# First expert's gate and up weights multiplied whole in float32; the slots for parts filled from the second expert's gate on

## The chip, the cores and the metric

The kernel runs on one core of a Trainium2 chip. Times are microseconds of device time for one execution; three runs of the kernel before gave a median of 1385.62 us (1385.28 to 1387.55). A difference between two kernels is stated with its sign, minus for faster.

The engines are named as in the profile: PE (matrix products, TensorE), DVE (VectorE), ACT (ScalarE), POOL (GpSimd), SP (SyncE, which issues DMAs). A matrix product accumulates in PSUM. The two levels of TensorE's clock are 2.4 and 1.2 GHz; a granted clock of 1.00 in the profile is the higher one, 0.50 the lower.

## The reference

Two layers of an encoder over 512 tokens of width 1024. Each layer is an attention part (four kinds of heads, their outputs joined and multiplied by `w_out`, added to `x`) and a mixture of 16 experts, of which each token uses two of one group. The experts' part is what the change touches:

```python
def hier_moe(h, wg, bg, we, be, w_gate, w_up, w_down):
    ...
    gate = jnp.sum(jax.nn.one_hot(expert_id, N_EXPERTS, dtype=jnp.float32) * (g_w * e_w)[..., None], axis=1)
    y = jnp.zeros_like(t)
    for e in range(N_EXPERTS):
        hid = jax.nn.silu(t @ w_gate[e]) * (t @ w_up[e])
        y = y + gate[:, e:e + 1].astype(t.dtype) * (hid @ w_down[e])
    return y.reshape(b, s, d)
```

`w_gate` and `w_up` are 1024x512 per expert, `w_down` 512x1024, all float32.

## The kernel before

**Precision in parts.** A float32 operand is cut into a high part (`hi`, an ACT copy into the rounded type fp32r) and a low part (`lo`, raw minus hi, on DVE or POOL): function `split` (L143 to L145). `mm3` (L264 to L269) then forms a product from three fp32r matmuls: hi times xh, lo times xh, hi times xl.

**Weights.** The class `Weights` streams all weights in pieces of 512 KB, numbered in the order of use. `load` (L183, L186) sends a piece into a raw room when one is free, on SP's queue; `split` turns the next loaded piece into parts when one of HL = 6 slots for parts is free, and gives its room back; `free` gives the slots back once the products have been issued. In a layer of the mixture the pieces follow `MOE_ORDER`: four of the first expert's gate, four of its up, four of the second's gate, four of the first's down, the second's up, the third's gate, and so on. In the tables of instructions, raw_1933, raw_3162, raw_3707 and raw_3709 are the first expert's gate in layer 0, raw_3711 to raw_3720 its up, and raw_3722 is the first piece of the second expert's gate.

**Experts.** Every expert works on at most CAP = 96 gathered tokens. For each, DVE makes four one-hot tiles (`oh`, L341), PE turns them into a list (`pli`, L1389), DVE reduces that to row numbers and weights, POOL gathers the rows (`xg`, L1401), PE turns them (`ptg`, L1413) and ACT and DVE split them into `xh` and `xl`. Then come gate (`pg`), up (`pu`), the product of both (`sg`), down (`pd`) and a scatter that adds to the output. The first expert's rows come another way: PE collects them while the attention ends (`acc`, L1142), and `turn` splits that straight from PSUM.

**What sets the order.** Towards the end of the attention a table, `TAIL`, says which steps are issued after which unit of work. Its words that matter here: `sV` and `sG` split the next piece on DVE or POOL if it is loaded and a slot is free (and do nothing otherwise), `c`, `o`, `d`, `e`, `f` with a digit are steps of the joined output and the router for a block of tokens, `T` is `turn` of the first expert, `K` the routing weights (24 small operations on DVE and two on ACT), `m` clears a buffer on POOL, `B` stores the last block of `x`, `S` gathers the second expert's rows, `O` is the branch for lists longer than CAP (not taken here), `q` copies constants on POOL. After the table the loop over `MOE_ORDER` issues the rest.

Of the kernel before, what the change touches and what calls it, by code (L numbers as in the profile page):

```python
# [11 lines left out]
FT = mybir.dt.float32  # L12
# [3 lines left out]
AF = mybir.ActivationFunctionType  # L16
# [3 lines left out]
S = 512  # L20
# [27 lines left out]
        69: "T K m sG B O q sG S"}  # L48
# [14 lines left out]
def hybrid_encoder(ctx: ExitStack, tc: tile.TileContext, I: dict, out: bass.AP, depth=2, dbg=None):  # L63
# [83 lines left out]
    class Weights:  # L147
# [4 lines left out]
        def __init__(self):  # L152
            self.spec, self.raw, self.hl, self.where = [], {}, {}, {}
            self.loaded = self.done = self.used = 0
            self.moe_pools = []
            self.held, self.paused = 0, False
            self.spare, self.spare_upto = [], 0

# [30 lines left out]

        def split(self, upto, E=V):  # L190

            while self.done < min(upto, self.loaded) and self.done < self.used + self.HL - self.held:
# [5 lines left out]
                r = self.where.pop(u)  # L198
                if isinstance(r, bass.AP):
                    self.spare.append(r)  # L200
# [13 lines left out]
        def free(self, upto):  # L214
            for u in range(self.used, upto):
                del self.hl[u]
            self.used = upto
# [25 lines left out]
    for l in range(depth):  # L243
# [10 lines left out]
        for e, m in MOE_ORDER:  # L254
# [3 lines left out]
            elif (e, m) == (NE - 1, 'u'):  # L258

                add_piece((l, e, m), I[src][l, e], 0, FF // 2, 8, 4, moe=True, parts=2, pairs=True)  # L260
            else:
                add_piece((l, e, m), I[src][l, e], 0, FF, 8, 2, moe=True, pairs=True)

# [59 lines left out]
    for layer in range(depth):  # L323
# [32 lines left out]
        with ExitStack() as c2:  # L356
# [431 lines left out]
            with ExitStack() as c3:  # L788
# [356 lines left out]
                def list_rows():  # L1145

                    pl = ps.tile([128, 512], FT, name="pli", tag="tr")
                    for t in range(NT):
# [7 lines left out]
                              p=route, x=pick, s=lambda E: W.split(W.done + 1, E), w=warm)  # L1156
# [151 lines left out]
        with ExitStack() as c2:  # L1308
# [69 lines left out]
            class Expert:  # L1378
# [25 lines left out]
                def turn(self, turned=None):  # L1404
                    self.xh = sm.tile([128, 8, CAP], FR, name="xh", bufs=2)
                    self.xl = sm.tile([128, 8, CAP], FR, name="xl", bufs=2)
                    for k in range(0, 8, 4):
                        if turned:
                            pt = turned[k // 4]
                        else:  # L1410
                            pt = ps.tile([128, 4, CAP], FT, name="ptg", tag="tr")
                            for j in range(4):
                                PE.transpose(pt[:, j], self.g[:CAP, (k + j) * 128:(k + j + 1) * 128], ident[:CAP, :CAP])  # L1413
                        split(self.xh[:, k:k + 4], self.xl[:, k:k + 4], pt)

                def gu(self, m, i, w):

                    if i == 0:
                        pool, tag = (pq, "pv") if m == 'u' else (ps, "mm") if self is not X[0] else (pq, "sc")
                        p = pool.tile([128, FF], FT, name="p" + m, tag=tag)  # L1420
                        setattr(self, 'p' + m, p[:CAP])
                    mm3(getattr(self, 'p' + m), [(self.xh[:, k], self.xl[:, k]) for k in (2 * i, 2 * i + 1)],
# [257 lines left out]
```

## Time and profile before

| | |
|---|---|
| median of three runs | 1385.62 us |
| the profiled execution | 1387.39 us, its span 1385.6 us |
| mean granted clock | 0.969 |
| busy, share of the span | PE 93%, DVE 78%, ACT 63%, POOL 26% |
| mixture stage, layer 0 | 386.8 to about 698 us |
| mixture stage, layer 1 | 1062.6 to about 1374 us |

A row of the timeline gives start, duration, engine, line, operation, output and inputs, how often in a row, and in brackets how long the engine had been idle before and what ended that. The durations of matmuls overlap, so one costs what lies between its start and the next one's. A float32 matmul stands in the trace as two records, an fp32r one as one.

### The profile page before, as it was taken

To read this page: it belongs to the slowest core of one execution; us is meant where nothing else is said; L and a number is where in the kernel's file an instruction comes from. 1 tells how busy PE (TensorE), PEld (TensorE's weight loads), DVE (VectorE), ACT (ScalarE), POOL (GpSimd) and SP (SyncE) were. 2 spreads that over 40 slices of the span, in tenths; PEclk is the share of its full clock that TensorE was granted. 3 is DMA by queue.
4 is the path that set the end of the run, shared out by engine and by line. 5 is a ranking of instruction groups with operands and counts; after the bars stand their busy time and mean duration, and the time that the engine had idled before them with its cause. 6 is when DMAs were issued, how large, how long until landed. Compare 5 with 4: busy or idle time off the path is not lost.

```text
span 1385.6 us, 21247 instructions
## 1 busy us (share of the span) xinstructions
PE 1293.8 (93%) x7222; PEld 1013.9 (73%) x7222; DVE 1087.5 (78%) x2108; ACT 876.4 (63%) x1439; POOL 358.5 (26%) x582
## 2 busy tenths in 40 slices
PE   8998899999969999999989998999998899999996
PEld 6776688888836666766777886888886566667674
DVE  4636776878688999999876488687876799999994
ACT  3443357766357888888744454676644588888884
POOL 4204324323422111111041152431345021111120
PEclk8999999999979999999999999999997899999999
DMA  7332251012699999999454223200176899999960
GB/s 198 116 97 62 83 177 51 18 60 108 257 334 292 370 363 373 359 361 332 124 136 123 91 77 79 69 28 28 62 296 222 292 351 368 370 363 366 367 206 13
DMA packets 100575, 278.46 MB, mean 201 GB/s; under 512 B 19465, under 2 KB 30521, under 8 KB 100456
## 3 DMA queue, kind: packets, MB, share of 16 engines
q1 hardware_dynamic: 89528, 247.95, 50.4%
q0 software_dynamic: 10352, 27.41, 7.9%
q10 hardware_dynamic: 576, 1.64, 0.4%
q8 instruction: 59, 0.97, 0.3%
q14 instruction: 60, 0.49, 0.1%
HBM read 264.34 MB, written 24.81 MB: 209 GB/s over the span
## 4 chain that ended last, share of the span: by engine, by line
PE 25%; DVE 17%; DMA 12%; issue 11%; ACT 4%; POOL 1%; POOLq 0%; DVEq 0%; ACTq 0%; SPq 0%
PE pm L268 9%; DVE lo L145 7%; PE pd L268 5%; DMA raw<-in_expert_w_down_dram 4%; DMA raw<-in_expert_w_gate_dram 3%; PE ptr L276 2%; DMA raw<-in_expert_w_up_dram 2%; PE pv L911 2%; PE pu L268 2%; ACT hi L144 2%; PE pg L268 2%; DMA out_dram<-ye,ix 1%; DVE oh L341 1%; ACT ye L1462 1%; DVE xl L145 1%
## 5 line engine op out<-in xcount | busy, mean ns | idle before, releaser
L145 DVE TENSOR_TENSOR lo<-raw,hi 128x1024 fp32r<-128x1024 f32 (+2 forms) x400 | 483.6, 1230 | 68.1 <-ACT hi L144 58.3
L144 ACT ACTIVATE hi<-raw 128x1024 fp32r<-128x1024 f32 (+1 forms) x410 | 422.7, 1050 | 92.6 <-PE pu L268 20.2
L268 PE MATMUL pm<-lo,hTh 128*128 128x512 f32 (+2 forms) x384 | 137.3, 358 | 6.8 <-DVE lo L145 5.1
L268 PE MATMUL pm<-hi,hTh 128*128 128x512 f32 (+2 forms) x384 | 139.3, 363 | 3.0 <-ACT hi L144 1.5
L268 PE MATMUL pm<-hi,hTl 128*128 128x512 f32 (+2 forms) x384 | 136.9, 356 | 0.4
L268 PE MATMUL pg<-lo,xh 128*96 128x512 f32 x256 | 104.0, 406 | 5.5 <-POOL lo L145 4.0
L268 PE MATMUL pu<-hi,xh 128*96 128x512 f32 (+1 forms) x272 | 109.0, 401 | 0.0
L268 PE MATMUL pg<-hi,xh 128*96 128x512 f32 x256 | 106.2, 415 | 2.4 <-ACTq L1478 1.4
L268 PE MATMUL pd<-hi,hl 128*96 128x512 f32 x256 | 102.1, 399 | 4.5 <-DVE hl L145 4.5
L268 PE MATMUL pu<-lo,xh 128*96 128x512 f32 (+1 forms) x272 | 105.7, 388 | 0.0
L268 PE MATMUL pu<-hi,xl 128*96 128x512 f32 (+1 forms) x272 | 104.8, 385 | 0.0
L911 PE MATMUL pv<-v,pT 128*128 128x64 f32 x768 | 98.3, 271 | 6.5 <-DVE pT L899 2.7
L268 PE MATMUL pg<-hi,xl 128*96 128x512 f32 x256 | 102.9, 402 | 0.6 <-DVE E L1349 0.6
L268 PE MATMUL pd<-lo,hh 128*96 128x512 f32 x256 | 101.2, 395 | 1.6 <-DVE lo L145 1.6
L882 ACT ACTIVATE p<-p,m 128x512 f32<-128x512 f32 x96 | 68.7, 716 | 52.2 <-DVE m L864 51.9
L911 PEld LDWEIGHTS pv<-v,pT 128*128 128x128 f32 x768 | 93.5, 192 | 10.8 <-DVE pT L899 4.8
L268 PE MATMUL pd<-hi,hh 128*96 128x512 f32 x256 | 100.7, 394 | 0.0
L268 PEld LDWEIGHTS pm<-lo,hTh 128*128 128x128 f32 x384 | 73.5, 191 | 18.2 <-DVE lo L145 9.8
L268 PEld LDWEIGHTS pm<-hi,hTh 128*128 128x128 f32 x384 | 73.8, 192 | 15.4 <-ACT hTh L144 2.4
L268 PEld LDWEIGHTS pm<-hi,hTl 128*128 128x128 f32 x384 | 73.5, 192 | 11.2 <-DVE hTl L145 2.1
L276 PE MATMUL ptr<-ident,p 128*128 128x128 f32 x512 | 76.9, 272 | 0.3
L276 PEld LDWEIGHTS ptr<-ident,p 128*128 128x128 f32 x512 | 63.3, 140 | 17.8 <-DVE pT L899 1.2
(371 smaller groups left out, 2746.6 us busy)
## 6 DMA issues: line engine op xcount, KB each, us to landing
raw<-in_expert_w_down_dram SPq DMA_DIRECT2D x116, 512.0 KB
raw<-in_expert_w_gate_dram SPq DMA_DIRECT2D x114, 512.0 KB
raw<-in_expert_w_up_dram SPq DMA_DIRECT2D x112, 512.0 KB
raw<-in_w_in_dram SPq DMA_DIRECT2D x32, 512.0 KB
raw<-in_w_out_dram SPq DMA_DIRECT2D x16, 512.0 KB
toep<-brep SPq DMA_DIRECT2D x16, 448.0 KB
x_sb<-in_expert_w_gate_dram SPq DMA_DIRECT2D x14, 512.0 KB
x_sb<-in_expert_w_down_dram SPq DMA_DIRECT2D x12, 512.0 KB
```

Source lines behind the costliest of these rows:

```text
L144: A.activation(hi, src, AF.Copy)
L145: E.tensor_tensor(lo, src, hi.bitcast(FT), op=OP.subtract)
L268: PE.matmul(pt, a, b, start=first and n == 0, stop=last and n == tot - 1)
L276: PE.transpose(pt[:c, i * 128:(i + 1) * 128], s, ident)
L341: V.tensor_scalar(oh[:, t], iota, pos[:, t, e:e + 1], None, op0=OP.is_equal)
L882: A.activation(p, p, AF.Exp, bias=m, scale=-1.0, accum_out=s)
L911: PE.matmul(st['pv'][:, t], self.pT[:, k * 128:(k + 1) * 128], self.v(k), start=k == 0, stop=k == NT - 1)
L1462: A.activation(ye[:CAP, n * 512:(n + 1) * 512], self.pd[n], AF.Copy, scale=self.w)
```

## The change

The first expert's eight gate and up pieces are put in a set `whole`: they are never split, take no slot for parts, and are multiplied as they are by the float32 copy of the first expert's rows, two float32 matmuls a piece. `turn` for that expert makes one copy of each half (ACT and DVE) and no low part. Their raw rooms are given back when their products have been issued. All splits before and in the first expert's stretch go to the pieces from the second expert's gate on; the words of the last row of `TAIL` are put in another order, with six `sV` and no `sG`.

```diff
--- before.py
+++ after.py
@@ -45,7 +45,7 @@
         66: "e1 sG c2",
         67: "f0 b3G o2 p0 r1V f1 h1 d2 o3 r2G e2 x0 p1 c3 d3 f2 e3 h30 x1 r3G p2 h2 f3",
         68: "x2 h31 p3 l x3",
-        69: "T K m sG B O q sG S"}
+        69: "m S T B sV sV sV sV sV sV K O q"}
 WAITP = 5
 JOIN = 52
 STORES = ((13, 0, 1), (6, 1, 2), (1, 2, 3), (0, 3, 4))
@@ -155,6 +155,7 @@
             self.moe_pools = []
             self.held, self.paused = 0, False
             self.spare, self.spare_upto = [], 0
+            self.whole = set()
 
         def add(self, src, k, n, moe=False):
             self.spec.append((src, k, n, moe))
@@ -187,17 +188,31 @@
                 self.raw[u] = r
                 self.loaded += 1
 
+        def room_for(self):
+            return sum(u not in self.whole for u in range(self.used, self.done)) < self.HL - self.held
+
+        def next(self):
+
+            while self.done in self.whole and self.done < self.loaded:
+                src, k, n, moe = self.spec[self.done]
+                self.hl[self.done] = self.raw.pop(self.done).rearrange("p (k n) -> p k n", k=k)
+                self.done += 1
+            return self.done
+
+        def leave(self, u):
+            r = self.where.pop(u)
+            if isinstance(r, bass.AP):
+                self.spare.append(r)
+
         def split(self, upto, E=V):
 
-            while self.done < min(upto, self.loaded) and self.done < self.used + self.HL - self.held:
+            while self.next() < min(upto, self.loaded) and self.room_for():
                 u = self.done
                 src, k, n, moe = self.spec[u]
                 hi = wp.tile([128, 1024], FR, name="hi", bufs=self.HL)[:, :k * n]
                 lo = wp.tile([128, 1024], FR, name="lo", bufs=self.HL)[:, :k * n]
                 split(hi, lo, self.raw.pop(u), E)
-                r = self.where.pop(u)
-                if isinstance(r, bass.AP):
-                    self.spare.append(r)
+                self.leave(u)
                 self.hl[u] = (hi.rearrange("p (k n) -> p k n", k=k), lo.rearrange("p (k n) -> p k n", k=k))
                 self.done += 1
                 self.load(len(self.spec))
@@ -214,6 +229,9 @@
         def free(self, upto):
             for u in range(self.used, upto):
                 del self.hl[u]
+                if u in self.whole:
+                    self.leave(u)
+                    self.load(len(self.spec))
             self.used = upto
 
     W = Weights()
@@ -260,6 +278,8 @@
                 add_piece((l, e, m), I[src][l, e], 0, FF // 2, 8, 4, moe=True, parts=2, pairs=True)
             else:
                 add_piece((l, e, m), I[src][l, e], 0, FF, 8, 2, moe=True, pairs=True)
+                if e == 0:
+                    W.whole.update(wbase[l, e, m][0])
 
     def mm3(pt, lhs, ws, first=True, last=True):
         n, tot = 0, 3 * len(ws)
@@ -1153,7 +1173,7 @@
                     X[1] = bass.IndirectOffsetOnAxis(ap=ix[:CAP], axis=0)
 
                 STAGES = dict(l=list_rows, b=norm_pair, c=turn_pair, o=open_out, d=close_out, e=turn_x, r=norm_x, f=logits, h=normed,
-                              p=route, x=pick, s=lambda E: W.split(W.done + 1, E), w=warm)
+                              p=route, x=pick, s=lambda E: W.split(W.next() + 1, E), w=warm)
 
                 def tail(words):
                     for w in words.split():
@@ -1403,14 +1423,17 @@
 
                 def turn(self, turned=None):
                     self.xh = sm.tile([128, 8, CAP], FR, name="xh", bufs=2)
+                    if turned:
+
+                        self.xh = self.xh.bitcast(FT)
+                        A.activation(self.xh[:, :4], turned[0], AF.Copy)
+                        V.tensor_copy(self.xh[:, 4:], turned[1])
+                        return
                     self.xl = sm.tile([128, 8, CAP], FR, name="xl", bufs=2)
                     for k in range(0, 8, 4):
-                        if turned:
-                            pt = turned[k // 4]
-                        else:
-                            pt = ps.tile([128, 4, CAP], FT, name="ptg", tag="tr")
-                            for j in range(4):
-                                PE.transpose(pt[:, j], self.g[:CAP, (k + j) * 128:(k + j + 1) * 128], ident[:CAP, :CAP])
+                        pt = ps.tile([128, 4, CAP], FT, name="ptg", tag="tr")
+                        for j in range(4):
+                            PE.transpose(pt[:, j], self.g[:CAP, (k + j) * 128:(k + j + 1) * 128], ident[:CAP, :CAP])
                         split(self.xh[:, k:k + 4], self.xl[:, k:k + 4], pt)
 
                 def gu(self, m, i, w):
@@ -1419,6 +1442,11 @@
                         pool, tag = (pq, "pv") if m == 'u' else (ps, "mm") if self is not X[0] else (pq, "sc")
                         p = pool.tile([128, FF], FT, name="p" + m, tag=tag)
                         setattr(self, 'p' + m, p[:CAP])
+                    if self is X[0]:
+                        for j in range(2):
+                            k = 2 * i + j
+                            PE.matmul(getattr(self, 'p' + m), self.xh[:, k], w[:, j], start=k == 0, stop=k == 7)
+                        return
                     mm3(getattr(self, 'p' + m), [(self.xh[:, k], self.xl[:, k]) for k in (2 * i, 2 * i + 1)],
                         [(w[0][:, j], w[1][:, j]) for j in range(2)], first=i == 0, last=i == 3)
```

On SP, in the attention of layer 0, the loads of the mixture stage are issued in this order; but for line numbers both programs have these rows.

```order
L186 DMA raw_3162<-in_expert_w_gate_dram 128x1024
L186 DMA raw_3707<-in_expert_w_gate_dram 128x1024
L186 DMA raw_3709<-in_expert_w_gate_dram 128x1024
L186 DMA raw_3711<-in_expert_w_up_dram 128x1024
L186 DMA raw_3716<-in_expert_w_up_dram 128x1024
L186 DMA raw_3718<-in_expert_w_up_dram 128x1024
L186 DMA raw_3720<-in_expert_w_up_dram 128x1024
L186 DMA raw_3722<-in_expert_w_gate_dram 128x1024
```

Nothing moved on SP here; the rows tell which load each number is. On DVE the split after unit 64 (word `sV`) stands between the last attention rows and the additions to `x_sb` that follow the output products. Before:

```order
L893 SCALAR_TENSOR_TENSOR p_3626<-p2_2558,m_3630,p_3626 128x512
L145 TENSOR_TENSOR lo_3754<-raw_1933,hi_3753 128x1024
L1049 TENSOR_TENSOR x_sb_68<-x_sb_68,pm_3739 128x512
L1049 TENSOR_TENSOR x_sb_68<-x_sb_68,pm_3746 128x512
L899 COPY pT_3780<-ptr_3775 128x512
L988 RECIPROCAL den2_1618<-den2_1618 128x2
```

Now:

```order
L913 SCALAR_TENSOR_TENSOR p_3626<-p2_2558,m_3630,p_3626 128x512
L145 TENSOR_TENSOR lo_3754<-raw_3722,hi_3753 128x1024
L1069 TENSOR_TENSOR x_sb_68<-x_sb_68,pm_3739 128x512
L1069 TENSOR_TENSOR x_sb_68<-x_sb_68,pm_3746 128x512
L919 COPY pT_3780<-ptr_3775 128x512
L1008 RECIPROCAL den2_1618<-den2_1618 128x2
```

The place is the same; the piece is raw_3722 instead of raw_1933. ACT's copy of the same piece moves with it.

On PE at the start of the mixture stage of layer 0 the first gate products were, before:

```order
L268 MATMUL pg<-hi,xh 96x512
L268 MATMUL pg<-lo,xh 96x512
L268 MATMUL pg<-hi,xl 96x512
L268 MATMUL pg<-hi,xh 96x512
L268 MATMUL pg<-lo,xh 96x512
L268 MATMUL pg<-hi,xl 96x512
```

Now, from the branch `O` to the first list product:

```order
L1506 UNCONDITIONAL_BRANCH
L1448 MATMUL pg<-raw,xh 96x512 x8
L1448 MATMUL pu<-raw,xh 96x512 x2
L1409 LDWEIGHTS oh
L1409 MATMUL pli<-parts,oh 96x5
```

Eight float32 products of `pg` and two of `pu` take the place of 24 and 6.

On DVE around the same place two stretches differ. Ahead of the branch, where `K` begins, before and then now:

```order
L1151 TENSOR_REDUCE scr<-pli 96x1
L1152 TENSOR_SCALAR nrd<-scr 96x1
L145 TENSOR_TENSOR xl<-acc,xh 128x384 x2
L1341 TENSOR_REDUCE mxg<-lg 128x4
L1343 TENSOR_TENSOR ge<-lg,mxg 128x16
L1349 SCALAR_TENSOR_TENSOR E_4310<-rank,goh 128x16 x4
```

```order
L1172 TENSOR_SCALAR nrd<-scr 96x1
L1430 COPY xh<-acc 128x384
L145 TENSOR_TENSOR lo<-raw,hi 128x1024 x5
L1361 TENSOR_REDUCE mxg<-lg 128x4
L1363 TENSOR_TENSOR ge<-lg,mxg 128x16
```

Five low parts come ahead of `K`, and a copy takes the place of two low parts of `x`. Behind the branch, before and then now:

```order
L1478 UNCONDITIONAL_BRANCH
L145 TENSOR_TENSOR lo<-raw,hi 128x1024 x5
L341 TENSOR_SCALAR oh<-iota,pos 128x96 x4
L145 TENSOR_TENSOR lo<-raw,hi 128x1024 x2
L341 TENSOR_SCALAR oh<-iota,pos 128x96 x4
L1392 TENSOR_REDUCE row<-pli 96x1
L1393 TENSOR_SCALAR ix<-row 96x1
L1397 TENSOR_REDUCE w<-pli 96x1
L341 TENSOR_SCALAR oh<-iota,pos 128x96 x4
```

```order
L1506 UNCONDITIONAL_BRANCH
L361 TENSOR_SCALAR oh<-iota,pos 128x96 x8
L1412 TENSOR_REDUCE row<-pli 96x1
L1413 TENSOR_SCALAR ix<-row 96x1
L1417 TENSOR_REDUCE w<-pli 96x1
L361 TENSOR_SCALAR oh<-iota,pos 128x96 x4
L1412 TENSOR_REDUCE row<-pli 96x1
L1413 TENSOR_SCALAR ix<-row 96x1
L1417 TENSOR_REDUCE w<-pli 96x1
L145 TENSOR_TENSOR xl<-ptg,xh 128x384 x2
```

The low parts that stood before and between the one-hot rows are gone from there.

## Rows read from the trace of the kernel before

**Rows 1.** Busy time by stretch: stretch, length, busy time per engine, PEclk, DMA share, GB/s.

```profile
386.80:419.30 32.50, 21.32 (x72) 13.32 (x73) 26.14 (x63) 16.32 (x19) 8.52 (x7) 0.71 0.89 324
419.30:680.00 260.70, 258.46 (x1254) 181.50 (x1253) 240.60 (x313) 215.76 (x257) 39.92 (x26) 1.00 0.96 338
1062.60:1094.10 31.50, 22.54 (x72) 13.89 (x73) 25.71 (x63) 16.76 (x20) 8.55 (x7) 0.66 0.88 319
```

**Rows 2.** Waits of PE, 386 to 420 us: total, times, longest.

```profile
PE pli L1389 <- DVE oh L341: 6.8, 3, 3.3
PE pg L268 <- POOL lo L145: 2.0, 2, 1.7
PE pg L268 <- DVE lo L145: 1.5, 1, 1.5
```

**Rows 3.** Timeline of PE, first expert's gate, layer 0.

```profile
386.78 0.71 PE L268 MATMUL pg<-hi,xh 128*96 128x512 f32 x1 [0.84 <-PEq L1478]
...
387.72 0.63 PE L268 MATMUL pg<-hi,xl 128*96 128x512 f32 x1
388.14 0.63 PE L268 MATMUL pg<-hi,xh 128*96 128x512 f32 x1
...
396.69 0.39 PE L268 MATMUL pg<-hi,xh 128*96 128x512 f32 x1
396.92 0.39 PE L268 MATMUL pg<-lo,xh 128*96 128x512 f32 x1
```

**Rows 4.** Timeline of DVE, same stretch.

```profile
386.98 0.16 DVE L1341 TENSOR_REDUCE mxg<-lg 128x4 f32<-128x16 f32 x1
...
390.62 2.38 DVE L1336 TENSOR_TENSOR first<-gate,parts 128x64 f32<-128x64 f32 x1
393.03 3.17 DVE L1334 CAST parts<-first 128x64 bf16<-128x64 f32 x1
...
396.56 0.26 DVE L1334 CAST parts<-first 128x64 bf16<-128x64 f32 x1
397.96 5.77 DVE L145 TENSOR_TENSOR lo<-raw,hi 128x1024 fp32r<-128x1024 f32 x5 [1.14 <-DVEq L1478]
403.64 0.80 DVE L341 TENSOR_SCALAR oh<-iota,pos 128x96 bf16<-128x96 f32 x4
```

**Rows 5.** Timeline of POOL, same stretch.

```profile
390.56 2.35 POOL L145 TENSOR_TENSOR lo<-raw,hi 128x1024 fp32r<-128x1024 f32 x1 [7.48 <-ACTq L1478]
...
393.68 2.40 POOL L145 TENSOR_TENSOR lo<-raw,hi 128x1024 fp32r<-128x1024 f32 x1
```

**Rows 6.** Groups by form, PE: line, operation, count, busy us, mean ns, idle before.

```profile
L911 PE MATMUL pv<-vm,pT 128*128 128x64 f32 x256 | 32.6, 270 | 4.2 <-DVE pT L899 3.2 <-DVE y L917 0.8
...
L1142 PE MATMUL acc<-scr,h 128*128 128x96 f32 x128 | 17.6, 296 | 0.0
```

**Rows 7.** Timeline of PE, a run of float32 matmuls.

```profile
375.50 1.92 PE L1142 MATMUL acc<-scr,h 128*128 128x96 f32 x16
```

**Rows 8.** Timeline of SP's queue, layer 0's attention.

```profile
337.06 1.75 SPq L186 DMA_DIRECT2D raw<-in_expert_w_up_dram  x4
338.85 2.41 SPq L186 DMA_DIRECT2D raw<-in_expert_w_gate_dram  x4
```

**Rows 9.** Busy time by stretch behind those issues, columns as in rows 1.

```profile
337.06:341.36 4.30, 4.09 (x17) 3.00 (x17) 4.13 (x10) 1.83 (x4) 1.91 (x4) 1.00 0.78 265
341.36:345.05 3.69, 3.46 (x22) 2.92 (x21) 2.41 (x7) 1.45 (x4) 2.47 (x11) 1.00 1.00 403
```

**Rows 10.** Timelines of ACT, DVE and PE at the split after unit 64, layer 0.

```profile
337.82 1.07 ACT L144 ACTIVATE hi<-raw 128x1024 fp32r<-128x1024 f32 x1
...
340.15 1.22 DVE L145 TENSOR_TENSOR lo<-raw,hi 128x1024 fp32r<-128x1024 f32 x1
341.83 0.69 DVE L1049 TENSOR_TENSOR x_sb<-x_sb,pm 128x512 f32<-128x512 f32 x1 [0.47 <-PE pm L268]
343.23 0.69 DVE L1049 TENSOR_TENSOR x_sb<-x_sb,pm 128x512 f32<-128x512 f32 x1 [0.71 <-PE pm L268]
...
344.78 0.48 PE L268 MATMUL pm<-hi,mh 128*128 128x512 f32 x1
```

## The prediction

> **What bounds the kernel now.** I read the slices of the page first, then busy time by stretch, and then followed the first expert's stretch and the tail of the attention row by row.
>
> Over the two mixture stages PE is the bound nearly everywhere: from the second expert on it is busy 258.46 of 260.70 us at the full granted clock [rows 1]. The exception is the stretch of the first expert, from its first gate matmul to the first gate matmul of the second: 32.50 us in layer 0 and 31.50 in layer 1, with PE busy 21.32 and 22.54 of it at a mean granted clock of 0.71 and 0.66 [rows 1]. Those 48 products of 512 columns cost .2295 us each, start to start, at the higher level of the clock (396.69 to 396.92), and .4255 at the lower (387.72 to 388.14) [rows 3]: 11.0 us of 32.5 if nothing were in the way. PE waits for three things there: low parts made on POOL (2.0 us) and on DVE (1.5), and the one-hot rows that turn the token lists into indices (6.8 in three waits, the longest 3.3) [rows 2]. All three are DVE's queue: it does the routing weights (24 small operations from 386.98 to 396.82), then five low parts in 5.77 us, then the one-hots, and more low parts between them [rows 4]. Two of the small operations take 2.38 and 3.17 us, where others of their kind take .26 [rows 4], and they stand beside the two low parts on POOL at 390.56 and 393.68, of 2.35 and 2.40 us [rows 5].
>
> So the change touches the one stretch of the stage where PE is not the bound. What is saved there lasts: after it PE and DVE run in a fixed rhythm (258.46 and 240.60 of 260.70 busy [rows 1]), neither with room to catch up or to fall behind.
>
> **Part 1, the products of the first expert.** 48 matmuls on parts become 16 float32 ones. The trace has no float32 matmul of 512 columns. It shows each narrow one as two records. From below: if a record costs no more per column than a part's product, a matmul is 2 x .2295 = .46 us. From above: the 16 records of 96 columns at 375.50 take 1.92 us [rows 7], .12 each, and if all of that were columns, 512 of them would be .64 and a matmul 1.28. Between: records of 64 columns average 270 ns and of 96 columns 296 [rows 6], .8 ns per column, so .42 us for 512 columns and .84 per matmul; I take .9 (at the lower clock 1.8). At the higher clock 16 x .9 = 14.4 us against 48 x .2295 = 11.0: the products get dearer by 3.4.
>
> The Trainium skill ("FP8 and Floating Point Precision", TensorE Precision Notes) says that true FP32 takes 4 passes through the array, and the three products replaced here would then be cheaper than the one that takes their place. By it a matmul is an estimate of 4 x .2295 = .92 us, and the sum moves by 16 x .02, under half a microsecond per layer; no run here shows 512 columns.
>
> **Part 2, what PE waits for.** The gate now needs only raw weights, long landed, and the plain copy of the gathered rows: its 3.5 us of waits for low parts [rows 2] go. DVE now does the copy (.56), five low parts (5.77), the routing weights, and then the one-hots at once. The routing weights took 9.84 us; without POOL's low parts beside them the two long operations fall to .26 each, so 9.84 - 2.38 - 3.17 + .52 = 4.8. From the gate's start (T0) that is about 10.5; the branch behind it costs .2 to 1.1; four one-hots .8 [rows 4]; the first list product stands at T0 + 11.8. PE meanwhile has eight gate and two up matmuls: 9.0 us at the higher clock, more when part of it falls at the lower one, so it ends near 10.1 to 11.8 too, and its wait there is short. Then eight one-hots and two short reductions, with the second list at 13.7 to 14.5; two up matmuls (16.3), the turn of the second expert's rows (17.3), two more (19.05), the last lists (21.3), the last two (23.1). The clock fell to the lower level wherever PE waited in this stretch [rows 1, 3]; up to 4 us more, of which I take 2: 25.1 from T0 to the second expert's gate. The gain is 32.5 - 25.1 = 7.4 in layer 0 and 31.5 - 25.1 = 6.4 in layer 1, together **13.8**, with ends at 10 (clock low most of the time) and 18 (never).
>
> Eight high copies fewer on ACT, six low parts fewer on DVE and two on POOL cost and give nothing beyond this: ACT and POOL are not waited for afterwards, and from the second expert's gate the six slots are full in both programs. POOL's gather of the second expert's rows, now ahead of the last store and the branch, comes earlier than its need near T0 + 16. SP's six loads that move ahead of its branch are for units some 26 places ahead and hide there. The whole units hold their rooms until their products are done, about 10 us longer than a split one; loads then issued are as far ahead, so nothing.
>
> **Part 3, a wait that comes in earlier.** The early split at word `sV` of unit 64 took the first gate piece, which had been loaded far ahead. It now takes the ninth piece of the stage (raw_3722), the fifth of the loads that SP issues from 337.06 on, when a room comes free: four up pieces, then four gate pieces from 338.85 [rows 8]. Five pieces are 2.62 MB. 265 GB/s for 4.30 us and 403 GB/s for 3.69 [rows 9] are 2.63 MB: the piece lands at 345.05 at the earliest. ACT reached the split at 337.82 and DVE at 340.15, where neither waited for weights [rows 10]. Now ACT copies from 345.5 to 346.6 and DVE subtracts to 347.8. Queued behind on DVE are the two additions to `x_sb` that empty PSUM (341.83 and 343.23 [rows 10]), and PE's next output products (344.78) need that PSUM. The additions now start at 347.75 and 348.35; DVE is 5.05 us late, as it had nothing to spare behind them, and PE, which had slack of .65 there, 4.4. From here PE is the bound to the end of the tail, and cannot make it up. If the idle 4 us drop the clock, 12 products at the lower level lose 12 x .196 = 2.4; PE was busy 4.09 of 4.30 before [rows 9], so I take .7. That is 5.1 per layer. Layer 1 has the same code and the same loads: **10.2** for both, with ends at 8.5 (no clock loss, a little slack) and 14.
>
> **The sum.** -13.8 + 10.2 = -3.6 us. The profiled execution spans 1385.6 and took 1387.39 with what lies around it; the median of the timed runs is 1385.62. I set the difference against the median: **1382 us**.
>
> **Rivals.**
> - The wait of part 3 does not bite: the gate piece lands sooner, or the slack takes it. For it: SP's queue is only that long because of one late room, and DVE and ACT would only meet it if the wait for the room is the same as before. Against: the split is reached 1.3 us after the issue [rows 8, 10], and the bytes ahead alone need 7. All of the gain stays: 1385.6 - 13.8 = 1372.
> - The wait is worth more than the gain, by the landing notice. The windows show when bytes move, not when a waiting engine is told. The piece was bounded by bytes alone; if the notice comes 2 us behind, each layer loses 2 more, and with the smaller gain of 10 the sum is -10 + 14.2 = 4.2, 1390. It decides from a stall of 5 us per layer on, if the gain is at its low end. The Trainium skill ("DMA: Bandwidth & Descriptors", Anatomy of one DMA) gives a fixed part of about 2.0 us per transfer, setup and completion together, for the GpSimd path; that these loads from SP have it too no row shows.
> - The float32 products are as dear as their upper bound, 1.28: 2 x 16 x .38 = 12.2 more than in my sum, 1394, slower. For it: nothing in the trace bounds the columns better than by averages of records. Against: the slope of rows 6.
> - The stretch's gain is given back later, because the loads or DVE set the rhythm of the stage rather than PE: only the stalls are left, 1385.6 + 10.2 = 1396. Against: PE is 99% busy there [rows 1]. DMA's share is 0.96 in that stretch, which speaks for it.
> - The change does next to nothing on both counts: 1385.
>
> **How the numbers follow.** My forecast .62 (its own range 1376 to 1388: faster .35, same .22, slower .05, the last being the second rival); the wait does not bite .17 (all faster); dear products .09 (slower .06, same .03); gain given back .07 (slower); next to nothing .05 (same .04, faster .01). Faster by over 0.2% .53, within 0.2% .29, slower .18; 0.2%, 2.8 us, is about what a measurement of this kernel can tell from no change. The range is 1374 to 1391: it leaves out part of the first rival, the dearest of the products and the gain given back, together a little under 2 in 10.
>
> **What would show it.** Right: ACT idle some 7 us before the copy of a gate piece near 338, released by that transfer, with PE idle some 4 us ahead of the output products that were at 344.78; `pg<-raw,xh` records .43 to .46 us apart at the higher clock; no operation of the routing weights over 1 us; no low parts on POOL; 25 us from the first gate to the second expert's gate, and the same rhythm after it. Wrong: no such idle time (then 1372), records at .6 or more (then slower), or a rhythm in the rest of the stage that is longer than before.

## The result and the profile after

The changed kernel takes 1396.65 us (median of 7 runs, 1393.2 to 1404.13), the kernel before beside it 1387.55 (7 runs, 1385.28 to 1390.85): a ratio of 1.0074, interval 1.0051 to 1.0096. It is slower by 0.7%, where 1382 was forecast. The profiled execution has a span of 1391.4 us, 5.8 above that of before; at 1393.2 us it is the fastest of the seven, so it shows about two thirds of the 9.1 us between the medians.

Three places in a layer mark where the time goes: the first output product of the token block at which the early split stands (P, 336.87 in layer 0 of before), the first gate product of the first expert (T0) and the first gate product of the second (G1). All numbers are differences of starts on PE, in us.

| | P to T0, layer 0 | T0 to G1, layer 0 | P to T0, layer 1 | T0 to G1, layer 1 |
|---|---|---|---|---|
| before | 49.9 | 32.6 | 50.9 | 31.5 |
| after | 56.9 | 28.3 | 58.5 | 27.7 |
| difference | +7.0 | -4.3 | +7.6 | -3.8 |

The four differences make +6.5; what lies before, between and behind them makes -0.7 (-1.0 up to the first P, +0.6 between the layers, -0.3 at the end).

**The early split.** The timeline of SP's queue, ACT, DVE and PE in the changed kernel, at the places of [rows 8, 10]:

```profile
336.06 1.75 SPq L187 DMA_DIRECT2D raw<-in_expert_w_up_dram  x4
337.85 2.03 SPq L187 DMA_DIRECT2D raw<-in_expert_w_gate_dram  x4
...
344.88 1.06 ACT L144 ACTIVATE hi<-raw 128x1024 fp32r<-128x1024 f32 x1 [7.93 <-DMA raw<-in_expert_w_gate_dram]
...
345.97 1.23 DVE L145 TENSOR_TENSOR lo<-raw,hi 128x1024 fp32r<-128x1024 f32 x1 [6.74 <-ACT hi L144]
347.11 1.28 DVE L1069 TENSOR_TENSOR x_sb<-x_sb,pm 128x512 f32<-128x512 f32 x2
...
347.85 0.80 PE L288 MATMUL pm<-hi,mh 128*128 128x512 f32 x1 [4.27 <-DVE x_sb L1069]
```

ACT sits 7.93 us until the gate piece has landed, DVE 6.74 behind ACT, and PE 4.27 behind the additions. The copy starts 8.82 us after SP's first issue. PE goes on behind the first of the two additions, before the second has ended. The windows of the changed kernel around it (columns as in rows 1) show how fast the bytes came, and the rest of the price:

```profile
336.06:344.13 8.07, 7.30 (x38) 5.64 (x36) 3.00 (x9) 0.89 (x3) 3.51 (x14) 1.00 0.87 332
...
344.00:348.00 4.00, 0.15 (x1) 0.16 (x1) 2.03 (x3) 1.17 (x2) 0.00 (x0) 0.92 1.02 412
348.00:352.00 4.00, 4.00 (x12) 3.17 (x13) 3.44 (x17) 2.19 (x9) 1.11 (x6) 0.65 1.03 411
352.00:356.00 4.00, 4.00 (x24) 3.35 (x23) 3.42 (x12) 1.23 (x3) 1.75 (x8) 1.00 0.56 224
...
360.00:364.00 4.00, 4.00 (x18) 3.42 (x19) 1.94 (x10) 0.59 (x4) 1.30 (x7) 0.63 0.84 290
```

332 GB/s over 8.07 us are 2.68 MB, a little more than the five pieces (2.62), so the gate piece is there by 344.13 and ACT's copy follows about 0.8 us later. After the idle 4 us the granted clock is 0.65 (part of the window at the lower level), and after eight us at or near 1.00 it falls once more, to 0.63, though PE was idle for only 0.25 us in between. In the kernel before, the windows of this stretch show 1.00 throughout. Run 7 below has the second fall without the pause.

**The first expert's stretch.** PE in the changed kernel, layer 0, in answer to [rows 3]:

```profile
392.78 7.08 PE L1448 MATMUL pg<-raw,xh 128*96 128x512 f32 x16 [1.00 <-DMA raw<-in_expert_w_down_dram]
404.23 3.70 PE L1448 MATMUL pu<-raw,xh 128*96 128x512 f32 x4 [4.37 <-DVEq L1506]
407.72 0.45 PE L1409 MATMUL pli<-parts,oh 128*96 128x5 bf16 x4
408.85 0.78 PE L1409 MATMUL pli<-parts,oh 128*96 128x5 bf16 x4 [0.68 <-DVE oh L361]
...
418.09 0.74 PE L1409 MATMUL pli<-parts,oh 128*96 128x3 bf16 x4 [2.80 <-DVE oh L361]
...
421.08 1.42 PE L288 MATMUL pg<-hi,xh 128*96 128x512 f32 x1
```

Eight gate products are 16 records. The first starts at 392.78 and the last at 399.26, so they stand .432 us apart, and a matmul costs .86 (the 7.08 us of the row hold the whole of the last record, which overlaps what follows). Two waits are there that before did not have: the first up product waits 4.37 us for DVE's branch, and a late list product 2.80 for its one-hots. ACT and DVE in the same stretch, in answer to [rows 4]:

```profile
392.44 5.80 DVE L145 TENSOR_TENSOR lo<-raw,hi 128x1024 fp32r<-128x1024 f32 x5
401.86 0.23 DVE L1356 TENSOR_TENSOR first<-gate,parts 128x64 f32<-128x64 f32 x1
402.12 0.26 DVE L1354 CAST parts<-first 128x64 bf16<-128x64 f32 x1
...
416.52 1.02 DVE L145 TENSOR_TENSOR xl<-ptg,xh 128x384 fp32r<-128x384 f32 x2 [6.45 <-ACT xh L144]
...
414.22 1.28 ACT L1455 ACT_TABLE_LOAD   x1 [14.03 <-SPq L1506]
415.51 0.59 ACT L1455 ACTIVATE sg<-pg 96x512 f32<-96x512 f32 x1
416.01 0.86 ACT L144 ACTIVATE xh<-ptg 128x384 fp32r<-128x384 f32 x2
```

The two operations of the routing weights that took 2.38 and 3.17 us are back to .23 and .26. But ACT stands still for 14.03 us behind the branch before the first expert's silu (`sg<-pg`), and what is queued behind the silu, the copy `xh` of the second expert's rows, comes 2.6 us after PE has turned them; DVE's `xl` and the one-hots follow. The waits of SP's queue in this stretch have this row for the branch itself:

```profile
SPq L1506 <- SPq L1506: 12.3, 7, 2.9
```

SP stands 12.3 us at the branch, in seven waits that no other engine ends. The trace has the semaphores of these waits: they are those of the loads that SP had issued from 396.16 us on, one after the other, and the last of them is passed at 414.11. The core's transfer rate from 396 to 416 us, in 40 slices, agrees:

```profile
GB/s 410 393 352 221 311 360 393 369 344 287 360 254 246 320 303 320 320 369 418 434 393 410 418 401 393 426 418 418 410 336 295 180 188 115 107 49 33 0 106 172
```

The loads that were moved ahead of the branch run out at 414 us; SP goes on at 414.2, and ACT's silu with it.

### The profile page after: what moved, and what is told of

The parts are those of the page before. It is cut to its first block, busy times and chain, and to the rows that moved or that the text cites. A ratio compares the mean times of both kernels' runs of the same rounds, so it can differ in the third digit from the quotient of the medians.

```text
span 1391.4 us, 21105 instructions
## 1 busy us (share of the span) xinstructions
PE 1295.8 (93%) x7190; PEld 1007.3 (72%) x7190; DVE 1061.3 (76%) x2094; ACT 856.5 (62%) x1419; POOL 348.6 (25%) x578
## 3 DMA queue, kind: packets, MB, share of 16 engines
q1 hardware_dynamic: 89816, 249.00, 49.9%
## 5 line engine op out<-in xcount | busy, mean ns | idle before, releaser
L145 DVE TENSOR_TENSOR lo<-raw,hi 128x1024 fp32r<-128x1024 f32 (+1 forms) x388 | 468.7, 1230 | 78.5 <-ACT hi L144 71.2
L144 ACT ACTIVATE hi<-raw 128x1024 fp32r<-128x1024 f32 (+1 forms) x394 | 406.4, 1050 | 112.4 <-PE pg L288 24.4
L288 PE MATMUL pu<-hi,xh 128*96 128x512 f32 (+1 forms) x256 | 100.1, 391 | 0.0
L288 PE MATMUL pg<-hi,xh 128*96 128x512 f32 x240 | 98.3, 409 | 0.0
L288 PE MATMUL pu<-lo,xh 128*96 128x512 f32 (+1 forms) x256 | 97.3, 380 | 0.0
L288 PE MATMUL pu<-hi,xl 128*96 128x512 f32 (+1 forms) x256 | 96.5, 377 | 0.0
L288 PE MATMUL pg<-lo,xh 128*96 128x512 f32 x240 | 94.8, 395 | 0.0
L288 PE MATMUL pg<-hi,xl 128*96 128x512 f32 x240 | 93.9, 391 | 0.0
```

The lines of the kernel that those rows point to most:

```text
L144: A.activation(hi, src, AF.Copy)
L145: E.tensor_tensor(lo, src, hi.bitcast(FT), op=OP.subtract)
L288: PE.matmul(pt, a, b, start=first and n == 0, stop=last and n == tot - 1)
```

## The experiments

Fourteen kernels in four groups; a ratio is to the kernel before on the same chip, so across groups the ratios compare better than the medians. The places P, T0 and G1 are as above, in the one profiled execution of each kernel. In layer 0 without the early split P to T0 is 49.5 to 49.7 us, or 50.6 to 51.1 where the clock falls once on the way (runs 7, 10, 11 and 13); no run shows that such a difference is the edit's.

| edit | median us | ratio, interval | P to T0, layers 0, 1 | T0 to G1, layers 0, 1 |
|---|---|---|---|---|
| 1 no early split | 1383.58 | 0.9959, 0.9943 to 0.9975 | 49.6, 50.7 | 29.9, 29.0 |
| 2 loads behind the branch | 1388.28 | 0.9993, 0.9974 to 1.0012 | 57.3, 56.9 | 25.6, 21.6 |
| 3 up products in another PSUM tile | 1399.92 | 1.0069, 1.0044 to 1.0094 | 57.0, 57.0 | 29.7, 30.7 |
| 4 order alone, all in parts | 1400.64 | 1.0079, 1.0052 to 1.0105 | 49.9, 50.9 | 36.4, 37.5 |
| 5 edits 1 and 2 | 1374.11 | 0.9907, 0.9889 to 0.9925 | 49.6, 50.7 | 25.2, 24.8 |
| 6 edits 1, 2 and 3 | 1373.35 | 0.9892, 0.9872 to 0.9913 | 49.5, 51.0 | 23.9, 23.9 |
| 7 no early split, splits in the loop | 1383.84 | 0.9970, 0.9953 to 0.9987 | 51.1, 50.7 | 28.3, 28.0 |
| 8 no early split, row of before | 1370.48 | 0.9878, 0.9855 to 0.9900 | 49.6, 50.7 | 22.4, 24.3 |
| 9 early split, row of before | 1383.20 | 0.9961, 0.9947 to 0.9976 | 57.1, 58.3 | 22.2, 23.3 |
| 10 as 8, two low parts on DVE | 1376.68 | 0.9913, 0.9896 to 0.9930 | 50.9, 50.7 | 25.5, 26.1 |
| 11 as 8, other PSUM tile | 1375.72 | 0.9906, 0.9886 to 0.9926 | 51.0, 50.7 | 21.7, 24.8 |
| 12 silu in another tile | 1383.46 | 0.9976, 0.9961 to 0.9991 | 57.5, 58.4 | 21.8, 23.8 |
| 13 as 10, both other tiles | 1366.45 | 0.9841, 0.9819 to 0.9863 | 50.6, 50.7 | 20.7, 22.2 |
| 14 as 8, silu in another tile | 1371.76 | 0.9890, 0.9875 to 0.9904 | 49.7, 50.9 | 22.3, 24.4 |

**1. No early split.**

```diff
-        64: "sV d0",
+        64: "d0",
```

> The changed kernel without the split after unit 64; the second expert's first gate piece is then split with the others in the table's last row. Theory A (three new waits: the early split waits for its piece, the silu waits for loads issued ahead of the branch, the first up product waits for DVE at the branch): the early split costs 6.9 + 7.6 = 14.5 us over both layers, of which one more low part ahead of the routing weights takes back 1.15 a layer: 12 us less than the changed kernel, about 1384.5, with the idle 4 us of PE ahead of the output products gone. Rival B (the float32 products and the low clock beside them are what costs): within 3 us of the changed kernel. Rival C (the new order of the last row costs, not the early split): within 3 us as well.

1383.58 us, P to T0 as before; the stretch behind it is 1.6 and 1.3 us longer, with one low part more. The windows of this run, in place of those after the wait above, with no fall of the clock:

```profile
347.00:351.00 4.00, 4.00 (x23) 3.35 (x23) 3.27 (x21) 1.73 (x9) 1.76 (x9) 1.00 1.02 419
...
359.00:363.00 4.00, 4.00 (x25) 3.27 (x24) 3.40 (x16) 0.14 (x2) 2.69 (x11) 1.00 0.48 135
```

Up to T0 the early split costs 7.3 and 7.8 us, both falls of the clock included. Theory A stands here. In the ten layers with the pause (changed kernel, runs 2, 3, 9 and 12) P to T0 is 56.9 to 58.5 us, whether the clock falls twice behind it or once and for longer.

**2. Loads behind the branch.** `z` holds the loads back, `u` lets them go.

```diff
-        69: "m S T B sV sV sV sV sV sV K O q"
+        69: "m S T B z sV sV sV sV sV sV K O u q"
```

> The changed kernel with the weight loads that the last row's splits release issued behind the branch instead of ahead of it; order of the splits unchanged. Theory A: ACT's first instruction behind the branch no longer waits for them (14 us of wait in layer 0 falls to a few), the list products lose their last wait (2.8 and 3.7 us), so about 6 us less than the changed kernel, 1390.5. Rival B: no change. Rival D (these loads are needed early, and moving them back starves the stage): slower than the changed kernel by 2 or more.

1388.28, a larger gain than expected: the stretch falls by 2.7 and 6.1. ACT's waits in layer 0:

```profile
ACT xh L144 <- PE ptg L1436: 7.3, 1, 7.3
ACT L1455 <- DVEq L1506: 3.9, 1, 3.9
```

The silu waits 3.9 us for DVE, no longer 14 for SP, and the copy of the rows waits for PE again, as it should.

**3. Another PSUM tile for the first expert's up products.**

```diff
-                        pool, tag = (pq, "pv") if m == 'u' else (ps, "mm") if self is not X[0] else (pq, "sc")
+                        pool, tag = (pq, "sc") if self is X[0] else (pq, "pv") if m == 'u' else (ps, "mm")
```

> The changed kernel with the first expert's up products accumulated in another PSUM tile, one that the branch does not use. Theory A: the wait of the first up product for DVE (4.4 and 3.7 us) goes, but the last list product still waits for the rows that ACT copies after its own wait, so the second expert's gate starts at nearly the same time: 0 to 2 us less, 1395 to 1397. Rival C' (that wait is the main loss of the stretch): 8 us less, 1388.5.

1399.92, no gain, and above the 1395 to 1397 of theory A; the interval reaches over the changed kernel's. PE's waits, layer 0 (the row for DVE's branch is gone):

```profile
PE pli L1409 <- DVE oh L361: 7.4, 3, 5.7
```

The wait for DVE had the next one behind it (the list products waited 3.5 us for one-hots in the changed kernel, 7.4 here): a wait that is not the last costs nothing.

**4. The new order alone**, in the kernel before.

```diff
-        69: "T K m sG B O q sG S"}
+        69: "m S T B sV sV sV sV sV sV K O q"}
```

> The kernel before with the new last row alone: all weights still in parts, no low parts on POOL, the early split takes the first gate piece as before. Theory A: no wait at unit 64; POOL's 2 to 3 us operations on DVE's routing weights go and the gate's low parts come early, but the silu waits for loads ahead of the branch: between 1381 and 1388. Rival C (the new order is the loss): 1392 or more.

1400.64, outside what theory A gave. The number is rival C's; the trace tells why, in the timeline of layer 0:

```profile
408.55 1.28 ACT L1427 ACT_TABLE_LOAD   x1 [6.93 <-SPq L1478]
409.85 0.59 ACT L1427 ACTIVATE sg<-pg 96x512 f32<-96x512 f32 x1
410.34 1.99 ACT L144 ACTIVATE hi<-raw 128x1024 fp32r<-128x1024 f32 x2
...
411.42 1.22 DVE L145 TENSOR_TENSOR lo<-raw,hi 128x1024 fp32r<-128x1024 f32 x1 [6.88 <-ACT hi L144]
412.56 0.80 DVE L341 TENSOR_SCALAR oh<-iota,pos 128x96 bf16<-128x96 f32 x4
```

It is the silu's wait again, with more behind it than I had counted: two high copies, DVE's low part, and the one-hots (PE waits 10.2 us for these). That it is the silu's tile here too was not tried in this kernel. Beside whole weights the same order costs no less (runs 8 and 9).

**5 and 6. The edits together.**

> The changed kernel with both waits taken away that the first runs showed: no split after unit 64, and the loads of the last row's splits issued behind the branch. Theory A (the waits add up): the first run's 1383.6, less the difference that the loads' place made to the first expert's stretch in the second run (28.3 to 25.6 in layer 0, 27.7 to 21.6 in layer 1; a low part more in the row takes 1.15 back in each): about 1376. Rival (what is won in the stretch is given back by loads that come too late for the second expert): 1382 or more.

> The same with the first expert's up products in a PSUM tile that the branch does not use, so that they no longer wait for DVE. Theory A: the list products still wait for DVE's one-hots behind five or six low parts and the routing weights, so 1 to 4 us less than the kernel without that: 1372 to 1375. Rival (that wait is hidden by the next): the same within 1.5 us.

1374.11, 2 us below theory A's figure: both waits add up. The third edit makes it 1373.35, inside the ranges of theory A and of the rival; the intervals overlap, so its worth stays unclear.

**7. Splits in the loop.**

```diff
-        64: "sV d0",
+        64: "d0",
...
-        69: "m S T B sV sV sV sV sV sV K O q"}
+        69: "m S T B K O q"}
```

> The changed kernel with no split after unit 64 and none in the last row of the table: the second expert's pieces are split one by one in the loop over the experts, behind the branch, and so are the loads that follow. Theory A: DVE is at the branch 6 us after the gate's start, the first up product does not wait, the silu waits for nothing, and the stretch is near its products, 19 to 22 us a layer: 1363 to 1369. Rival D (low parts late: the second expert's gate waits for them, as DVE has 93% to do from then on and cannot catch up): 1376 or more.

1383.84, a miss by some 15 us, and not for rival D's reason. The timeline of layer 0:

```profile
403.88 1.28 ACT L1455 ACT_TABLE_LOAD   x1 [10.67 <-SPq L1506]
405.17 0.59 ACT L1455 ACTIVATE sg<-pg 96x512 f32<-96x512 f32 x1
405.66 1.99 ACT L144 ACTIVATE hi<-raw 128x1024 fp32r<-128x1024 f32 x2
...
406.74 1.23 DVE L145 TENSOR_TENSOR lo<-raw,hi 128x1024 fp32r<-128x1024 f32 x1 [8.91 <-ACT hi L144]
407.88 0.80 DVE L361 TENSOR_SCALAR oh<-iota,pos 128x96 bf16<-128x96 f32 x4
```

Loads that were issued ahead of the branch anyway still hold SP, and with it the silu, until 403.88, 12 us from the gate's start. Every split behind the branch queues behind the silu on ACT, and its low part stands ahead of one-hots on DVE. The splits were better placed ahead of the branch, their loads behind it (run 5, 1374.11).

This run has no pause at unit 64, and yet the clock falls where it fell for the second time in the changed kernel, about 32 us ahead of T0 in both:

```profile
356.00:360.00 4.00, 3.75 (x35) 3.51 (x33) 1.03 (x5) 3.09 (x9) 1.36 (x1) 0.99 0.83 330
360.00:364.00 4.00, 4.00 (x12) 3.19 (x13) 2.47 (x10) 0.33 (x2) 2.76 (x10) 0.58 0.50 158
```

Layer 0 of runs 10 and 11 and layer 1 of runs 6 and 14 have it too, all without the early split; the other layers without the pause do not. So the second fall does not need the pause.

**8 and 9. The row of before, without and with the early split.**

```diff
-        69: "m S T B sV sV sV sV sV sV K O q"}
+        69: "T K m sG B O q sG S"}
```

> The first expert's weights whole, with the table of the kernel before but for the split after unit 64, which is left out: low parts on POOL as before, few loads ahead of the branch. It is the products' part of the change alone. Theory A: the gate's waits go, one wait for DVE at the branch of about 4 us comes, the two long operations of the routing weights stay: stretch 25 to 27 us a layer, 1376. Rival B (whole float32 products do not pay, 3.4 us dearer a layer): 1388 or more.

> The changed kernel with the last row of the table as in the kernel before, the split after unit 64 in place. With the three kernels already run (changed 1396.7; no early split 1383.6; neither early split nor new row 1370.5) it is the fourth corner. Theory A: the early split costs what it cost beside the new row, 13 to 15 us: 1383.5 to 1385.5. Rival (the early split is harmful only because of what the new row does later): within 4 us of 1370.5.

1370.48 and 1383.20. Run 8 is 5.5 us better than forecast: its stretch is 22.4 and 24.3 us, not 25 to 27, with a wait for DVE at the branch of 2.4 us in layer 0, not 4; rival B is out. Run 9 is 0.3 us below the range of its theory A. With run 1 and the changed kernel this is a square. By the ratios the early split costs 1.15% beside the new row and 0.83% beside the old one (16 and 12 us), the new row 1.13% beside the early split and 0.81% without it, each known to about 4 us. The marks agree: the early split costs 7 to 8 us a layer up to T0 beside either row, the new row 4 to 8 us a layer behind T0. Each does its harm alone, and without both the whole weights bring 1.2%. In run 8, layer 0, POOL's low parts still stretch the routing weights, and the silu waits (the row names the one-hots, but by the trace SP passes its branch at 401.3 as well), but it ends a microsecond before the rows are turned that ACT copies next:

```profile
391.31 2.21 DVE L1356 TENSOR_TENSOR first<-first,parts 128x64 f32<-128x64 f32 x1
393.56 3.14 DVE L1354 CAST parts<-first 128x64 bf16<-128x64 f32 x1
...
401.44 1.28 ACT L1455 ACT_TABLE_LOAD   x1 [8.02 <-DVE oh L361]
402.74 0.59 ACT L1455 ACTIVATE sg<-pg 96x512 f32<-96x512 f32 x1
404.36 0.87 ACT L144 ACTIVATE xh<-ptg 128x384 fp32r<-128x384 f32 x2 [1.03 <-PE ptg L1436]
```

**10 and 11. Run 8 with one more wait taken away each**: low parts on DVE behind the routing weights (10), the PSUM tile of run 3 (11).

```diff
-        69: "T K m sG B O q sG S"}
+        69: "T K sV sV m S B O q"}
```

> The best so far (whole weights, no early split, row of before: 1370.5) with its two low parts on POOL made on DVE behind the routing weights instead. Theory: the two long operations of the routing weights (2.21 and 3.14 us beside POOL's low parts) fall to .26 each and two low parts of 1.15 come, 2.6 us less on DVE ahead of the branch; the first up product's wait (2.4) goes, and the silu's wait for the landing of the loads, near 14 us from the gate's start, is then the next limit: 1366 to 1370. Rival (POOL's low parts cost nothing, since PE is busy with the gate beside them): 1370 to 1372.

> The best so far with the first expert's up products in the PSUM tile that the branch does not use. Theory: their wait for DVE (2.4 us) goes and the list products come up to 2 us earlier, behind the one-hots: 1366 to 1369.5. Rival (the next wait takes its place, as in the run with that edit alone): 1370 to 1372.

1376.68 and 1375.72, both above their theory and their rival: neither is faster than run 8, and 10 is slower. Of the difference 1.4 us are the fall of the clock ahead of T0 in both. Run 11's stretch is 21.7 and 24.8 us against 22.4 and 24.3, so its edit changes next to nothing there; run 10's is 3.1 and 1.8 longer. ACT in run 10, with SP's loads ahead of the branch (the `up` row) and behind it:

```profile
407.07 1.28 ACT L1455 ACT_TABLE_LOAD   x1 [12.13 <-SPq L1506]
...
394.25 3.12 SPq L187 DMA_DIRECT2D raw<-in_expert_w_up_dram  x3
407.06 1.76 SPq L187 DMA_DIRECT2D raw<-in_expert_w_gate_dram  x4
```

DVE was early, but the silu waited until 16.7 us from the gate's start. In run 8 it was 13.9. Run 10 has both of its splits ahead of the branch, where run 8 has one of them behind it, and so one load more stands ahead of it: the third of the `up` row, issued at 397.05, where run 8 issues its third at 401.43, behind the branch. That this load alone makes the difference was not tried.

**12. The first expert's silu in another tile.** The branch loads weights into `sg` from SP; `xl` it does not load.

```diff
-                    self.sg = sm.tile([128, FF], FT, name="sg", bufs=1)
+                    if self is X[0]:
+                        self.sg = sm.tile([128, 8, CAP], FR, name="xl", bufs=2).rearrange("p k n -> p (k n)")[:, :FF].bitcast(FT)
+                    else:
+                        self.sg = sm.tile([128, FF], FT, name="sg", bufs=1)
```

> The changed kernel with one edit: the first expert's silu writes a tile that SP never loads in the branch (an xl tile, which that expert no longer needs) instead of sg. Order, loads and splits are as in the changed kernel. Theory A: the silu waits for SP's loads only because the branch's code loads into sg, so its wait of 14 us goes with the loads still ahead of the branch, and the stretch is as short as in the run with the loads behind it: 1387 to 1391. Rival (no engine goes on behind the branch until SP is there, whatever tile it uses): 1394 to 1399.

1383.46, below the range of theory A and far from the rival's. Order, splits and loads are those of the changed kernel. ACT and PE, layer 0:

```profile
402.78 1.28 ACT L1458 ACT_TABLE_LOAD   x1 [0.86 <-DVE wt L1385]
404.45 0.59 ACT L1458 ACTIVATE xl<-pg 96x512 f32<-96x512 f32 x1 [0.39 <-PE pg L1448]
411.60 0.87 ACT L144 ACTIVATE xh<-ptg 128x384 fp32r<-128x384 f32 x2 [6.56 <-PE ptg L1436]
...
416.36 0.80 PE L288 MATMUL pg<-hi,xh 128*96 128x512 f32 x1
```

The silu runs right behind the gate, 14 us of wait are gone, and the stretch is 21.8 and 23.8 us. So the wait came from the shared tile alone: SP stands at its branch until 416.8 in this run, by the trace, and ACT has long passed it.

**13 and 14. All of it, and run 8 with the silu in another tile.**

> All the waits found taken away together: no early split, two low parts on DVE behind the routing weights, the up products in another PSUM tile, the silu in another tile. Theory A: nothing but the products, the lists and the turn is left in the stretch, 19 to 21 us a layer instead of 25.5 and 26.1: 1363 to 1368. Rival (the stretch is then bound by the second expert's low parts, split late): 1372 or more.

> The best so far (whole weights, no early split, row of before: 1370.5) with the silu in another tile alone. Theory A: its silu waited until 13.9 us from the gate's start, 3 us before the rows it holds up were needed; 1 to 3 us less: 1367 to 1370. Rival (the wait was hidden there): 1370 to 1372.

1366.45, a ratio of 0.9841 (0.9819 to 0.9863) to the kernel before: the lowest of all, though its interval overlaps that of run 8, and faster than the kernel before and the changed one. The stretch is 20.7 us in layer 0, as forecast, and 22.2 in layer 1, above the 19 to 21. PE's waits that are left in layer 0:

```profile
PE pli L1409 <- DVE oh L361: 2.2, 2, 1.5
PE pg L1448 <- DMA raw<-in_expert_w_down_dram: 0.3, 1, 0.3
```

Run 14 is as run 8: there the silu's wait was hidden, as that forecast's rival said.

## Why the prediction was wrong

- **The step that failed is the sentence of part 2 on SP's queue**: "SP's six loads that move ahead of its branch are for units some 26 places ahead and hide there." They are needed late, but they were moved ahead of a branch whose code loads into the tile that the silu writes. I asked when their data is used and not what waits for the queue that issues them. In place of the 25.1 us of the stretch stood 28.3 and 27.7; run 12, with nothing but the tile changed, has 21.8 and 23.8. That is 10.4 us over both layers. Run 12 also shows that the rest of part 2 was near: its sum was 23.1 before 2 us were added for the clock.
- **The wait of the first up product for DVE's branch** (4.37 us) was not in the working either. It is the same kind, a PSUM tile that the branch uses. In the changed kernel it is hidden by the silu's wait: run 3 takes it away and gains nothing.
- **Part 3 had the mechanism right, and its size too small**: 5.1 us a layer forecast, 7.0 and 7.6 measured. The copy came 8.82 us after the first issue, where 8.4 were worked out, and PE's idle 4 us were as forecast, though partly by luck: the working let PE wait for the second addition with .65 us of slack, and it went on behind the first, which was later but had more slack. The term that was mis-sized is the clock, .7 taken: in layer 0 PE lost 1.3 us in the first fall (4.1 late before the 12 products at 347.85, 5.4 behind them), and another 1.5 in a second fall that I had not thought of, with PE busy. The pause is not what the second fall needs (run 7); why it comes is open.
- **The prices in part 1 were right**: .86 us per float32 matmul of 512 columns where .9 was taken and the ends were .46 and 1.28. The Trainium skill ("FP8 and Floating Point Precision", TensorE Precision Notes) with its 4 passes gave an estimate of .92, and the trace agrees within 7%. The rival of dear products is out.
- **The routing weights** took what was forecast: no operation over a microsecond, and the first one-hots start 11.3 us from T0 (404.06), as worked out; the list behind them stood at 14.9 instead of 11.8: PE waited for DVE until 404.23 and then did two up products at the lower clock, in 3.70 us.
- **The rivals.** The second, "the wait is worth more than the gain", is right as a sentence, but not by its mechanism: the copy came about 0.8 us behind the bytes, not 2 or more beyond what was worked out. The Trainium skill ("DMA: Bandwidth & Descriptors", Anatomy of one DMA) has about 2.0 us fixed per transfer, setup and completion together, for the GpSimd path; for these loads, from SP, what stands behind the queued bytes is the 0.8. The fourth rival's time, 1396, is the one measured, but by chance: the gain was not given back behind the stretch (+0.6 us between the layers), part of it never came.
- **The range** ended at 1391, at a gain of 10 us with a stall of 14. Measured were 8.1 and 14.6: both terms lie a little beyond their dear ends. From 1382 to 1396.65 these two make 10.1 us; the kernel before was itself 1.9 slower beside the changed one, the medians differ by 3.3 more than the profiled executions, and 0.7 goes the other way. What the 3.3 are was not traced.

## What to carry to other kernels

When work moves past a branch or a loop on a DMA queue, ask what the branch's code writes and reads from each engine: in this kernel the first instruction behind it that touched such a tile waited for that engine's queue (runs 3 and 12), and that queue for the loads issued ahead (12.3 us). An early step put into a slot must be asked for its input's landing anew when the input changes, even if the step itself stays where it was. And what a wait is worth depends on what else stands in the way: the silu's own tile brings 10 us in the stretches of the changed kernel (run 12) and nothing in run 8 (run 14). Run 13, with both tiles, is 10 us faster than run 10; which of the two brings it was not tried.

## What the runs showed of the hardware

- PE's granted clock fell right behind a pause of 4.3 us (4.6 in layer 1): in the changed kernel to 0.65 in 348 to 352 us, with the first products .43 us apart instead of .23. It fell again to 0.63 in 360 to 364, after eight us of which PE was idle .25; the last thing PE did before were 16 narrow records (`pl`, 20 columns) in 2 us. Run 1, with neither pause nor fall, and run 7, with the second fall and no pause, show that the two are not one thing. Why the second comes in some of the profiled executions and not in others is open.
- A float32 matmul of 96 rows and 512 columns costs .86 us at the higher clock, as two records .43 apart, where an fp32r one costs .23.
- Five loads of 512 KB issued on SP from 336.06 to 338.4 us had the last one's reader running 8.82 us after the first issue; the core moved 332 GB/s over the first 8.07 of these.
- At a branch that is not taken SP waited 12.3 us for the landing of loads it had issued ahead. ACT, whose next instruction wrote a tile that SP does not load in the branch, passed it without that wait (run 12).
